# A two-layer hybrid encoder trunk on one core: four plain tiles in the channel mixers, with low parts of weights made by accumulating transfers

## The chip, the core and the metric

The kernel runs on one core of a Trainium2 chip. The core has a matrix engine (TensorE, "PE" in the profile, with its weight loads as "PEld"), a vector engine (VectorE, DVE), a scalar engine (ScalarE, ACT), a general engine (GpSimd, POOL) and a queue engine (SyncE, SP). Each runs its instructions in the order in which they stand, and they wait for each other on semaphores. Transfers are issued by SP, ACT or POOL and carried out by 16 DMA engines. The metric is device time in microseconds (us) of one execution; lower is better.

## What is computed

Batch 1, 512 tokens, width 1024, two layers, everything in float32. A layer is a token mixer and a channel mixer, each added to x. The part that matters here is the channel mixer, once per layer, and the final norm:

```python
def conv_ffn(h, w_up, conv_w, conv_b, w_down):        # h = rmsnorm(x, norm_ffn_g[l]), 512 x 1024
    u, g = jnp.split(h @ w_up, 2, axis=-1)            # w_up 1024 x 5632: u and g are 512 x 2816
    g = causal_dwconv(g, conv_w, conv_b)              # three taps along the tokens
    return (jax.nn.silu(g) * u) @ w_down              # w_down 2816 x 1024

x = x + conv_ffn(rmsnorm(x, norm_ffn_g[l]), ffn_w_up[l], ...)
...
return rmsnorm(x, final_g)                            # after the last layer
```

The first layer's token mixer is an mLSTM with memory attention, the second's a band attention with memory attention; neither is touched.

## The kernel before

Matrices are kept transposed: 128 features on the partitions, 512 tokens along the free axis. To reach float32 accuracy with a single-pass matmul type, each operand is split into a high part and a low part (`split`: ACT copies the high part, DVE subtracts it from the source), and each product is three matmuls (`mm3`, L194 to L196): high weights with high data, high weights with low data, low weights with high data. The low part of the weights is thus first needed by the third matmul.

The up projection's 2816 channels are 22 tiles of 128. Each has a "gate" and an "up" half, each with weights of 1024 x 128, loaded by SP into one of three raw buffers (`wr`), split into one of three pairs of buffers (`wh0`/`wl0` to `wh2`/`wl2`, here buffers 0, 1, 2; `weight_tiles` hands them out in turn, and `turn` may be moved on to skip some). There are two ways to do a tile:

- A *plain* tile (`plain`) multiplies all 8 feature blocks over all 512 tokens: 2 x 8 x 3 matmuls of 512 columns. The first three plain tiles use data that isn't yet scaled by the norm, and DVE scales the result by a row (L718); later ones use scaled data. Then come the three taps (ACT L692, DVE L685 twice), a Silu (L722), the product with the up half (L727) and the split of the result, which is kept in `hid`.
- A *block* tile (`step`) treats gate and up, and two halves of features and tokens, as a 2 x 2 block product in seven products of 256 columns instead of eight: 7 x 4 x 3 matmuls of 256 columns. It needs sums and differences of the data (`forms`, made once per mixer in four steps, one for each pair of feature blocks) and of the weights (`Forms`, made for each tile: `sums`, `split_second`, `sum_third` and so on).

The down projection is accumulated in DRAM in groups of four tiles of `hid` (`GROUP`): a *down unit* is 4 x 3 matmuls of 512 columns for one block of output features. Its sum is copied out of PSUM by ACT and added into `xspill` in DRAM by a transfer that accumulates (L778, issued by POOL). `UNITS` says which units are done beside which tile.

Before, tiles 0 to 4 are plain, and units 0 to 3 follow the fifth plain tile. The steps of `forms` (scaling of x, its splits, then the four sums) are woven into the plain tiles by `weave`, which calls the next step each time so many matmul triples have been written. All this is written in program order and then ordered by a scheduler; the block tiles after it stand under a manual schedule for PE, ACT and DVE, in the order written in `step`.

At the end of the program the second mixer's last six tiles are multiplied with the tokens on the partitions, and for each group T of 128 tokens `final_norm` scales the rows by the inverse root of their mean square (one Newton step after a square root) and issues two output transfers, one from ACT's queue and one from SP's.

Of the kernel before, what the change touches and what calls it, by code (L numbers as in the profile page):

```python
# [13 lines left out]
ALU = mybir.AluOpType  # L14
# [25 lines left out]

PLAIN, UNSCALED, GROUP, LAST = 5, 3, 4, 6
UNITS = {PLAIN - 1: (0, 1, 2, 3), 5: (None, 4), 6: (None, 5), 7: (None, 6), 8: (None, 7)}
UNITS.update((j, (2 * j - 10, 2 * j - 9)) for j in range(9, 21))

# [8 lines left out]
def trunk(  # L55
# [139 lines left out]
        nc.tensor.matmul(o, lh, rl, start=False, stop=False, skip_group_check=more)  # L195
        nc.tensor.matmul(o, ll, rh, start=False, stop=last, skip_group_check=more)  # L196

    def project(w, c0, act, tag="mm"):


        n = len(act)
        wh, wl = weights(rows(w, c0, P), n, P)
        o = ps(tag)
        for k in range(n):
            mm3(o, wh[:, k, :], wl[:, k, :], act[k][0], act[k][1], k == 0, k == n - 1)
            yield
        return o
# [457 lines left out]
    class ChannelMixer:  # L665
# [35 lines left out]
        def plain(self, j):  # L701
            scale = self.norm.row if j < UNSCALED else None
            act = self.act if j < UNSCALED else self.ready
            gate = project(self.w, DFF + j * P, act)
            up = project(self.w, j * P, act, "sc")
            if self.norm.row is None:
                both = pair_of(gate, up)
                weave(self.norm.finish(), both, 1)
                og, ou = yield from both
                scale = self.norm.row  # L710
            else:
                og = yield from gate
# [12 lines left out]
            if ou is None:  # L725
                ou = yield from up
            V.tensor_tensor(out=acc, in0=ou, in1=acc, op=ALU.mult)  # L727
            self.keep(acc)

        def forms(self):  # L730

            for j in range(KT):
                V.scalar_tensor_tensor(
                    xT[j], xT[j], self.gain[:, j : j + 1], self.norm.row, op0=ALU.mult, op1=ALU.mult
                )
                hi, lo = sb("u", [P, S], F32R), sb("u", [P, S], F32R)
                split(hi, lo, xT[j])
                self.ready.append((hi, lo))
                yield
            self.sums = []  # L740
            for k in range(KT // 2):
                b1, b2 = xT[k], xT[k + KT // 2]
                forms = []
                ta, tb = sb("t", [P, S]), sb("t", [P, S])
                for o, x, y in (
                    (ta[:, :H], b1[:, H:], b1[:, :H]),
                    (ta[:, H:], b2[:, H:], ta[:, :H]),
                    (tb[:, :H], b2[:, H:], b1[:, H:]),
                    (tb[:, H:], b2[:, :H], ta[:, H:]),
                ):  # L750
                    V.tensor_tensor(out=o, in0=x, in1=y, op=ALU.subtract)
                for t in (ta, tb):
                    for h in (t[:, :H], t[:, H:]):
                        both = sb("u", [P, S], F32R)
                        split(both[:, :H], both[:, H:], h)
                        forms.append(both)
                self.sums.append(forms)
                yield

# [6 lines left out]
        def down_products(self, u):  # L766
            g, j = divmod(u, KT)
            w = self.down[u // 2]
            o = ps("tr")
            c = slice(u % 2 * P, (u % 2 + 1) * P)  # L770
            for k in range(GROUP):
# [28 lines left out]

        def t(self, i):

            return [(p[i - 1][:, :H], p[i - 1][:, H:]) for p in self.sums]

        def later(self):


            prep, tail = Forms(self, PLAIN), None
            prep.split_up()
            prep.sums()  # L810
            prep.split_second()
            prep.sum_third()
            prep.split_sums()
            prep.sum_fourth()
# [619 lines left out]
    def add_squares(T, t):  # L1434

        if len(sums[T]) == 1:
            V.tensor_scalar(sums[T][0], sums[T][0], 1.0 / D, EPS, op0=ALU.mult, op1=ALU.add)
        elif sums[T]:
            last = sums[T].pop()
            V.scalar_tensor_tensor(sums[T][0], last, 1.0 / D, sums[T][0], op0=ALU.mult, op1=ALU.add)  # L1440
        sums[T].append(small(1))
        sq = sb("t", [P, S])
        A.activation(sq[:, : t.shape[-1]], t, AF.Square, accum_out=sums[T][-1])

    def final_norm(T):
        v, r, t = small(1), small(1), small(1)
        first, second = sums[T]
        A.activation(r, second, AF.Sqrt, scale=1.0 / D, bias=first)
        V.scalar_tensor_tensor(v, second, 1.0 / D, first, op0=ALU.mult, op1=ALU.add)
        V.reciprocal(r, r)  # L1450
        V.tensor_mul(t, r, r)
        V.scalar_tensor_tensor(t, t, -0.5, v, op0=ALU.mult, op1=ALU.mult)
        V.scalar_tensor_tensor(r, t, 1.5, r, op0=ALU.add, op1=ALU.mult)
        A.activation(xt[T][0], xt[T][0], AF.Copy, scale=r)
        nc.scalar.dma_start(out[T * P : (T + 1) * P, :S], xt[T][0])
        V.scalar_tensor_tensor(xt[T][1], xt[T][1], r, fgb[1], op0=ALU.mult, op1=ALU.mult)
        nc.sync.dma_start(out[T * P : (T + 1) * P, S:], xt[T][1])

    hid = channel_mixer(1, act, norm, col["gffn"][:, 8:16], lambda: None)
    n = LAST // 2  # L1460
# [77 lines left out]
```

## Time and profile before

| | us |
|---|---|
| median of 3 timed runs | 1179.51 (1179.32 to 1180.14) |
| profiled execution: its own time | 1181.13 |
| profiled execution: span from first to last instruction | 1179.4 |
| PE busy in that span | 1167.9 |
| DVE busy | 941.3 |
| ACT busy | 730.0 |
| POOL busy | 129.7 |

Rows of the timeline read: start, busy time, engine, line, operation, tiles written and read, shapes; in brackets the idle time before and what ended it. Matmuls are pipelined, so their starts tell the pace and not their lengths. Where a source line is a helper's (L140 and L141 are the two steps of `split`), the tiles and the place in time tell which use it is. `pmm`, `psc`, `ptr` are PSUM buffers; plain gates write `pmm`, plain ups `psc`, down units `ptr`.

### The profile page before, as it was taken

What the parts mean: (1) busy time and instruction counts of PE and PEld (TensorE: products, weight loads), DVE (VectorE), ACT (ScalarE), POOL (GpSimd) and SP (SyncE); (2) the same over time, 40 slices, a digit from 0 to 9 for tenths busy, and PEclk for the clock granted to TensorE, in tenths of its full rate; (3) what the DMA queues carried; (4) which work ended last, traced back from release to release, by engine and by line L of the source; (5) the groups of instructions that cost most, each with busy time, mean ns of one, the idle gap of its engine ahead of it and who ended that gap; (6) DMA issues with size and microseconds to landing.
All of it is one profiled execution on the core that took longest, in us unless ns stands there. A gap on an engine that the chain in (4) does not pass through costs nothing.

```text
span 1179.4 us, 18657 instructions
## 1 busy us (share of the span) xinstructions
PE 1167.9 (99%) x7007; PEld 1033.9 (88%) x7007; DVE 941.3 (80%) x1688; ACT 730.0 (62%) x1294; POOL 129.7 (11%) x222
## 2 busy tenths in 40 slices
PE   8999999999999999999999999999999999999997
PEld 8988888888889999999888888888889999999986
DVE  5877778787979877777697888897897887777755
ACT  5638578654656665556576667776565665666545
POOL 0211101000011111111021000101001011110100
PEclk9999999999999999999999999999999999999999
DMA  8645425244366866666564312335426466566551
GB/s 283 206 116 132 105 54 152 66 136 134 90 155 146 189 157 171 151 154 136 146 196 134 90 54 80 105 104 179 143 90 152 109 137 143 142 143 143 126 161 72
DMA packets 200156, 158.64 MB, mean 135 GB/s; under 512 B 8344, under 2 KB 179838, under 8 KB 200066
## 3 DMA queue, kind: packets, MB, share of 16 engines
q1 hardware_dynamic: 183906, 119.74, 34.7%
q0 software_dynamic: 15584, 36.67, 15.7%
q8 instruction: 55, 0.90, 0.3%
q10 hardware_dynamic: 576, 1.05, 0.2%
q14 instruction: 35, 0.29, 0.1%
HBM read 128.89 MB, written 32.46 MB: 137 GB/s over the span
## 4 chain that ended last, share of the span: by engine, by line
PE 93%; DVE 3%; DMA 2%; ACT 1%; SPq 1%; issue 0%; POOL 0%; POOLq 0%; ACTq 0%; DVEq 0%
PE pmm L194 18%; PE pmm L195 18%; PE pmm L196 18%; PE ptr L195 6%; PE ptr L194 6%; PE ptr L196 6%; PE psc L196 5%; PE psc L195 5%; PE psc L194 5%; PE psc L544 2%; PE ptr L1365 1%; DMA wr<-in_mem_w_kv_dram 1%; PE ptr L1386 1%; PE ptr L1387 1%; DMA u<-in_mem_dram 1%; PE ptr L627 1%
## 5 line engine op out<-in xcount | busy, mean ns | idle before, releaser
L194 PE MATMUL pmm<-u,wh 128*128 128x512 f32 (+1 forms) x968 | 333.0, 344 | 0.2 <-ACT u L140 0.2
L196 PE MATMUL pmm<-u,wl 128*128 128x512 f32 (+1 forms) x968 | 330.7, 342 | 0.0
L195 PE MATMUL pmm<-u,wh 128*128 128x512 f32 (+1 forms) x968 | 330.4, 342 | 0.0
L141 DVE TENSOR_TENSOR wl<-wr,wh 128x1024 fp32r<-128x1024 f32 (+3 forms) x172 | 199.9, 1163 | 81.6 <-ACT wh L140 81.2
L140 ACT CAST wh<-wr 128x1024 fp32r<-128x1024 f32 (+3 forms) x172 | 171.9, 1001 | 93.3 <-PE pmm L195 40.3
L196 PEld LDWEIGHTS pmm<-u,wl 128*128 128x128 f32 x968 | 181.9, 188 | 20.7
L194 PEld LDWEIGHTS pmm<-u,wh 128*128 128x128 f32 x968 | 181.8, 188 | 18.8 <-ACT u L140 1.1
L195 PEld LDWEIGHTS pmm<-u,wh 128*128 128x128 f32 x968 | 182.0, 188 | 18.4 <-DVE u L141 0.5
L194 PE MATMUL ptr<-u,wh 128*128 128x512 f32 x272 | 106.4, 391 | 0.0
L195 PE MATMUL ptr<-u,wh 128*128 128x512 f32 x272 | 106.2, 390 | 0.0
L196 PE MATMUL ptr<-u,wl 128*128 128x512 f32 x272 | 105.8, 389 | 0.0
L778 POOL DMA_DIRECT2D xspill<-t x64 | 55.5, 867 | 432.6 <-ACT t L777 420.1
L834 ACT COPY t<-pmm 128x256 f32<-128x256 f32 x102 | 38.2, 374 | 76.6 <-PE pmm L196 76.5
L141 DVE TENSOR_TENSOR u<-t,u 128x512 fp32r<-128x512 f32 (+1 forms) x94 | 54.3, 604 | 35.4 <-ACT u L140 35.4
L194 PE MATMUL pmm<-u,fh 128*128 128x256 f32 x272 | 75.4, 277 | 0.0
L195 PE MATMUL pmm<-u,fh 128*128 128x256 f32 x272 | 75.2, 277 | 0.0
L196 PE MATMUL psc<-u,wl 128*128 128x256 f32 (+1 forms) x232 | 75.1, 324 | 0.0
L196 PE MATMUL pmm<-u,fl 128*128 128x256 f32 x272 | 75.1, 276 | 0.0
L195 PE MATMUL psc<-u,wh 128*128 128x256 f32 (+1 forms) x232 | 75.1, 324 | 0.0
L194 PE MATMUL psc<-u,wh 128*128 128x256 f32 (+1 forms) x232 | 74.9, 324 | 0.0
L141 DVE TENSOR_TENSOR fl<-pt,fh 128x512 fp32r<-128x512 f32 x102 | 70.3, 689 | 5.1 <-ACT fh L140 1.4
L140 ACT CAST fh<-pt 128x512 fp32r<-128x512 f32 x102 | 62.9, 616 | 8.8 <-DVE pt L888 5.6
(335 smaller groups left out, 2510.4 us busy)
## 6 DMA issues: line engine op xcount, KB each, us to landing
wr<-in_ffn_w_up_dram SPq DMA_DIRECT2D x54, 512.0 KB, 6.5
wr<-in_ffn_w_down_dram SPq DMA_DIRECT2D x38, 512.0 KB, 5.3
pt<-in_ffn_w_up_dram SPq DMA_DIRECT2D x34, 512.0 KB, 8.0
xspill<-t POOLq DMA_DIRECT2D x64, 256.0 KB, 4.5
wr<-in_a_w_in_dram SPq DMA_DIRECT2D x20, 512.0 KB, 3.9
wr<-in_w_kv_dram SPq DMA_DIRECT2D x12, 512.0 KB, 4.1
xspill<-fh POOLq DMA_DIRECT2D x16, 256.0 KB, 2.6
xspill<-fl POOLq DMA_DIRECT2D x16, 256.0 KB, 2.8
```

The costliest lines, as they stand in the source:

```text
L140: high = A.copy(hi, src) if on_act else V.tensor_copy(hi, src)
L141: low = V.tensor_tensor(out=lo, in0=src, in1=f(hi), op=ALU.subtract)
L194: nc.tensor.matmul(o, lh, rh, start=first, stop=False, skip_group_check=more)
L195: nc.tensor.matmul(o, lh, rl, start=False, stop=False, skip_group_check=more)
L196: nc.tensor.matmul(o, ll, rh, start=False, stop=last, skip_group_check=more)
L544: nc.tensor.matmul(o, a, b, start=first and i == 0, stop=i == 1)
L627: nc.tensor.matmul(o2, vs[a][:, 2 * hp + h, :], p[h][:, a, :], start=i == 0, stop=i == 3)
L778: G.dma_start(xspill[j], t, accum_op=ALU.add)
L834: A.copy(o, r[:, :H])
L1365: nc.tensor.transpose(tp[:, b * P : (b + 1) * P], es[T, h][:, b * P : (b + 1) * P], ident)
L1386: nc.tensor.matmul(o2[:, s * P :], w, hi_at(pts[h], s, s, TT - s), start=s == 0, stop=False)
L1387: nc.tensor.matmul(o2[:, s * P :], w, lo_at(pts[h], s, s, TT - s), start=False, stop=s == TT - 1)
```

## The change

Five things change in the channel mixers and at the end:

1. `PLAIN` goes from 5 to 4: tile 4 becomes a block tile. Units 0 to 3 now follow tile 3, and tile 4 has no unit beside it.
2. For plain tiles 2 and 3 (gate and up, so four weight tiles a mixer), the low part is made by `added`: ACT copies the high part, then writes its negative into the low buffer, and POOL issues a transfer that reads the weights from DRAM a second time and adds them there. The raw buffer is free once the high part is copied.
3. Units 0 and 1 do their first three parts at once and their fourth, which needs tile 3's own result, later.
4. The last of the four sums of x is made after the first parts of tile 4's weights (`run(forms)` moves into `later`), and the results of the sums are split in 512 columns at a time instead of 256.
5. `final_norm` uses one small DVE step fewer, and the last group's rows are scaled and sent in two halves, three of the four transfers by SP.

The turn of the buffers changes too: `turn` is moved on once, ahead of tile 2.

```diff
-PLAIN, UNSCALED, GROUP, LAST = 5, 3, 4, 6
+PLAIN, UNSCALED, GROUP, LAST = 4, 3, 4, 6
...
+    def added(src, a, b):
+
+        hi, lo = weight_tiles(a, b)
+        A.copy(hi, load(src, a, b))
+        A.activation(lo, f(hi), AF.Copy, scale=-1.0)
+        G.dma_start(lo, src.bitcast(F32R), accum_op=ALU.add)
+        return hi, lo
+
-    def project(w, c0, act, tag="mm"):
+    def project(w, c0, act, tag="mm", split_by=weights):
...
-        wh, wl = weights(rows(w, c0, P), n, P)
+        wh, wl = split_by(rows(w, c0, P), n, P)
...
-            gate = project(self.w, DFF + j * P, act)
-            up = project(self.w, j * P, act, "sc")
+            gate, up = (
+                project(self.w, c0 + j * P, act, tag, added if j >= 2 else weights) for c0, tag in ((DFF, "mm"), (0, "sc"))
+            )
...
-                    for h in (t[:, :H], t[:, H:]):
-                        both = sb("u", [P, S], F32R)
-                        split(both[:, :H], both[:, H:], h)
-                        forms.append(both)
+                    hi, lo = sb("u", [P, S], F32R), sb("u", [P, S], F32R)
+                    split(hi, lo, t)
+                    forms += [(hi[:, c], lo[:, c]) for c in (slice(0, H), slice(H, S))]
...
-        def later(self):
+        def later(self, forms):
...
             prep.split_second()
+            run(forms)
             prep.sum_third()
...
-        skips = -(turn[0] + 1) % 3
+        skips = -(turn[0] + 2) % 3
         for j in range(1, UNSCALED):
-            turn[0] += j <= skips
+            turn[0] += skips * (j == UNSCALED - 1)
...
-            weave(mixer.plain(j), forms, 4 / (16.0 * (PLAIN - UNSCALED)))
+            weave(mixer.plain(j), forms, 3 / (16.0 * (PLAIN - UNSCALED)))
+            started = {}
             for u in units:
...
-                mixer.add(*mixer.down_products(u))
-        run(forms)
-        mixer.later()
+                if u < 2:
+                    started[u] = mixer.down_products(u, 0, GROUP - 1)[1]
+                if u == 1:
+                    for v, o in started.items():
+                        mixer.add(*mixer.down_products(v, GROUP - 1, GROUP, o))
+                if u >= 2:
+                    mixer.add(*mixer.down_products(u))
+        mixer.later(forms)
...
-        V.tensor_mul(t, r, r)
-        V.scalar_tensor_tensor(t, t, -0.5, v, op0=ALU.mult, op1=ALU.mult)
-        V.scalar_tensor_tensor(r, t, 1.5, r, op0=ALU.add, op1=ALU.mult)
...
+        V.scalar_tensor_tensor(t, r, v, r, op0=ALU.mult, op1=ALU.mult)
+        V.scalar_tensor_tensor(r, t, 3.0, r, op0=ALU.add, op1=ALU.mult)
+        step = S if T < TT - 1 else MEM
+        for c in range(0, S, step):
+            a, b = (t[:, c : c + step] for t in xt[T])
+            last = c + step == S
+            A.activation(a, a, AF.Copy, scale=r)
+            V.scalar_tensor_tensor(b, b, r, fgb[1][:, c : c + step], op0=ALU.mult, op1=ALU.mult)
+            nc.sync.dma_start(out[T * P : (T + 1) * P, S + c : S + c + step], b)
+            (nc.scalar if last else nc.sync).dma_start(out[T * P : (T + 1) * P, c : c + step], a)
```

How the instructions move is seen at two places of the first mixer. The digit after `wh` or `wl` is the buffer. On ACT, from the Silu of tile 0 on, before (`wh1613` is tile 2's gate, `wh0635` tile 3's gate, `wh2623` tile 2's up):

```order
L722 ACTIVATE t588_3033<-t588_3033 128x512
L140 CAST wh1613_3143<-wr612_3141 128x1024
L140 CAST u590_3042<-t588_3033 128x512
L140 CAST wh0635_3240<-wr634_3238 128x1024
L692 ACTIVATE t600_3087<-t601_3088,cols1_799 128x512
L140 CAST u596_3066<-fh448_2360 128x512
L140 CAST u598_3083<-fh449_2362 128x512
L140 CAST wh2623_3192<-wr622_3190 128x1024
L722 ACTIVATE t600_3087<-t600_3087 128x512
```

and now, the same stretch (`wh0612` is tile 2's gate, `wh1622` its up):

```order
L731 ACTIVATE t588_3033<-t588_3033 128x512
L201 CAST wh0612_3141<-wr614_3143 128x1024
L202 ACTIVATE wl0613_3142<-wh0612_3141 128x1024
L140 CAST u590_3042<-t588_3033 128x512
L700 ACTIVATE t600_3087<-t601_3088,cols1_799 128x512
L140 CAST u596_3066<-fh448_2360 128x512
L140 CAST u598_3083<-fh449_2362 128x512
L140 CAST u606_3115<-fh450_2364 128x512
L731 ACTIVATE t600_3087<-t600_3087 128x512
L140 CAST u608_3132<-fh451_2366 128x512
L201 CAST wh1622_3191<-wr624_3193 128x1024
L202 ACTIVATE wl1623_3192<-wh1622_3191 128x1024
```

Tile 3's gate no longer has its copy here. It stands further down, and its negative copy (`wl2637`) behind tile 2's tap (L700 on `t620`):

```order
L140 CAST u626_3212<-fl454_2372 128x512
L201 CAST wh2636_3244<-wr638_3246 128x1024
L700 ACTIVATE t620_3183<-t621_3184,cols1_799 128x512
L140 CAST u628_3229<-fl455_2374 128x512
L202 ACTIVATE wl2637_3245<-wh2636_3244 128x1024
L731 ACTIVATE t620_3183<-t620_3183 128x512
L201 CAST wh0647_3295<-wr649_3297 128x1024
L202 ACTIVATE wl0648_3296<-wh0647_3295 128x1024
```

The accumulating transfers follow each negative copy on POOL's queue, with nothing else between them; behind them come the down units' own. On PE, at the end of tile 1's up (`psc605`) and the start of tile 2's gate (`pmm615`), before:

```order
L194 MATMUL psc605_3101<-u571_2950,wh2603_3097 128x512
L195 MATMUL psc605_3101<-u572_2951,wh2603_3097 128x512
L196 MATMUL psc605_3101<-u571_2950,wl2604_3098 128x512
L194 MATMUL pmm615_3147<-u538_2794,wh1613_3143 128x512
L195 MATMUL pmm615_3147<-u539_2795,wh1613_3143 128x512
L196 MATMUL pmm615_3147<-u538_2794,wl1614_3144 128x512
```

and now:

```order
L194 MATMUL psc605_3101<-u571_2950,wh1603_3097 128x512
L195 MATMUL psc605_3101<-u572_2951,wh1603_3097 128x512
L196 MATMUL psc605_3101<-u571_2950,wl1604_3098 128x512
L194 MATMUL pmm615_3148<-u538_2794,wh0612_3141 128x512
L195 MATMUL pmm615_3148<-u539_2795,wh0612_3141 128x512
L196 MATMUL pmm615_3148<-u538_2794,wl0613_3142 128x512
```

The order of the matmuls is the same there; the buffers and what fills them are not. Tile 1's gate is in buffer 1 before and in buffer 0 now, so in both programs tile 2's gate takes the buffer that tile 1's gate has just left.

More of the change, by code (lines that the diff above doesn't have):

```diff
@@ L764, in load_down, with down_products @@
             return load(rows(ffn_w_down[self.l], 2 * jj * P, 2 * P, GROUP * g, GROUP * (g + 1)), GROUP, 2 * P)
-        def down_products(self, u):
+        def down_products(self, u, k0=0, k1=GROUP, o=None):
             g, j = divmod(u, KT)
             w = self.down[u // 2]
-            o = ps("tr")
+            o = o or ps("tr")
             c = slice(u % 2 * P, (u % 2 + 1) * P)
-            for k in range(GROUP):
+            for k in range(k0, k1):
                 mm3(o, w[0][:, k, c], w[1][:, k, c], *self.hid[GROUP * g + k], k == 0, k == GROUP - 1)
@@ L801, in t @@
         def t(self, i):
-            return [(p[i - 1][:, :H], p[i - 1][:, H:]) for p in self.sums]
-        def later(self):
+            return [p[i - 1] for p in self.sums]
+        def later(self, forms):
             prep, tail = Forms(self, PLAIN), None
@@ L1436, in add_squares @@
         if len(sums[T]) == 1:
-            V.tensor_scalar(sums[T][0], sums[T][0], 1.0 / D, EPS, op0=ALU.mult, op1=ALU.add)
+            V.tensor_scalar(sums[T][0], sums[T][0], 4.0 / D, 4 * EPS, op0=ALU.mult, op1=ALU.add)
         elif sums[T]:
             last = sums[T].pop()
-            V.scalar_tensor_tensor(sums[T][0], last, 1.0 / D, sums[T][0], op0=ALU.mult, op1=ALU.add)
+            V.scalar_tensor_tensor(sums[T][0], last, 4.0 / D, sums[T][0], op0=ALU.mult, op1=ALU.add)
         sums[T].append(small(1))
@@ L1447, in final_norm @@
         first, second = sums[T]
-        A.activation(r, second, AF.Sqrt, scale=1.0 / D, bias=first)
-        V.scalar_tensor_tensor(v, second, 1.0 / D, first, op0=ALU.mult, op1=ALU.add)
+        A.activation(r, second, AF.Sqrt, scale=4.0 / D, bias=first)
+        V.scalar_tensor_tensor(v, second, -4.0 / D, first, op0=ALU.mult, op1=ALU.subtract)
         V.reciprocal(r, r)
-        V.tensor_mul(t, r, r)
-        V.scalar_tensor_tensor(t, t, -0.5, v, op0=ALU.mult, op1=ALU.mult)
-        V.scalar_tensor_tensor(r, t, 1.5, r, op0=ALU.add, op1=ALU.mult)
[L1454 to L1457, printed above, removed]
+        V.scalar_tensor_tensor(t, r, v, r, op0=ALU.mult, op1=ALU.mult)
[8 more added lines that the diff above has]
+            (nc.scalar if last else nc.sync).dma_start(out[T * P : (T + 1) * P, c : c + step], a)
     hid = channel_mixer(1, act, norm, col["gffn"][:, 8:16], lambda: None)
```

## The prediction

> **What bounds the kernel now.** I read the page first, then the busy time by stages, then the timelines at the places where the change works. The page's first part and its chain of waits:
>
> ```profile
> span 1179.4 us, 18657 instructions
> PE 1167.9 (99%) x7007; PEld 1033.9 (88%) x7007; DVE 941.3 (80%) x1688; ACT 730.0 (62%) x1294; POOL 129.7 (11%) x222
> PE 93%; DVE 3%; DMA 2%; ACT 1%; SPq 1%; issue 0%; POOL 0%; POOLq 0%; ACTq 0%; DVEq 0%
> ```
>
> TensorE (PE) carries the span. A busy PE need not run at its peak, so here are stages of the first channel mixer (its tiles 0 to 2; tiles 3 and 4 with the four early down units; the blocks) and the end of the program. The columns are length, then busy time of PE, its weight loads, DVE, ACT and POOL, the granted clock, the DMA share and GB/s.
>
> ```profile
> 282.60:309.80 27.20, 27.20 (x122) 22.51 (x121) 26.54 (x38) 17.88 (x26) 0.00 (x0) 1.00 0.32 96
> 309.80:342.60 32.80, 32.80 (x145) 26.93 (x144) 30.18 (x58) 19.78 (x37) 2.59 (x3) 1.00 0.42 110
> 342.60:582.00 239.40, 239.40 (x1764) 225.39 (x1763) 190.76 (x275) 143.86 (x243) 39.42 (x53) 1.00 0.65 154
> 1172.20:1179.40 7.20, 0.19 (x2) 0.00 (x0) 2.05 (x9) 1.52 (x4) 0.00 (x0) 0.82 0.38 146
> ```
>
> The mixers leave PE no idle time. The matmuls also start at an even pace, which the timeline of PE shows: first a stretch of 512-column matmuls (24 for each weight tile, two weight tiles a plain tile), then of 256-column ones (84 a block).
>
> ```profile
> 298.90 0.39 PE L194 MATMUL pmm<-u,wh 128*128 128x512 f32 x1
> 299.13 0.39 PE L195 MATMUL pmm<-u,wh 128*128 128x512 f32 x1
> 299.35 0.39 PE L196 MATMUL pmm<-u,wl 128*128 128x512 f32 x1
> ...
> 304.34 0.39 PE L194 MATMUL psc<-u,wh 128*128 128x512 f32 x1
> ...
> 309.78 0.39 PE L194 MATMUL pmm<-u,wh 128*128 128x512 f32 x1
> ...
> 320.66 0.39 PE L194 MATMUL pmm<-u,wh 128*128 128x512 f32 x1
> ...
> 342.61 0.28 PE L194 MATMUL pmm<-u,wh 128*128 128x256 f32 x1
> ...
> 345.33 0.28 PE L194 MATMUL pmm<-u,fh 128*128 128x256 f32 x1
> ```
>
> From 298.90 to 304.34 lie 24 matmuls: 0.2267 us each. From 342.61 to 345.33 lie 24 of the narrow kind: 0.1133 each. So only two things move the time inside the mixers: the number of columns that PE streams, and any wait that the change brings in. There is no wait to take out.
>
> **Columns.** A plain tile is 48 x 0.2267 = 10.88 us, a block 84 x 0.1133 = 9.52. One tile of each of the two mixers changes from the one to the other: 2 x 1.36 = **2.72 us less**. The four early down units keep their 48 matmuls and only move one tile earlier.
>
> **The accumulating transfers.** For tiles 2 and 3 the low part no longer comes from DVE in one step. ACT writes the high part, then its negative, and POOL's queue adds the raw weights from DRAM. DVE loses four 1024-column steps a mixer, ACT gains four; neither is on PE's path, since PE ran without a gap beside them. What counts is when the low part is there: the third matmul of a weight tile needs it (L196). So the latency of the transfer, from issue to landing, stands on PE's path wherever the buffer comes free late. In the new order tile 2's gate of the first mixer takes buffer 0, last read by tile 1's gate, with one weight tile (5.44 us) between them. Before, it took buffer 1, last read by the same distance, but its chain was short. That wait for the buffer is in the trace of before, on ACT:
>
> ```profile
> 293.43 1.05 ACT L140 CAST wh<-wr 128x1024 fp32r<-128x1024 f32 x1 [1.05 <-PE pmm L195]
> ...
> 295.38 1.05 ACT L140 CAST wh<-wr 128x1024 fp32r<-128x1024 f32 x1
> 296.34 0.81 ACT L692 ACTIVATE t<-t,cols 128x512 f32<-128x512 f32 x1
> 297.05 1.12 ACT L140 CAST u<-fh 128x512 fp32r<-128x512 f32 x2
> ```
>
> A copy of 1024 columns holds ACT 0.96 us (295.38 to 296.34), the tap 0.71, a copy of 512 some 0.56. Let L be the latency of one transfer. High copy from 293.43, negative copy behind it, 0.1 to issue: 295.45. The low part lands at 295.45 + L, the matmul starts 0.1 later; today it starts at 299.35. The first wait is therefore L - 3.8. The remaining 22 matmuls take 4.99, so the gate ends at 300.5 + L. Now the second place: on ACT the negative copy for tile 3's gate stands behind tile 2's tap, which needs that gate's sum scaled by DVE. DVE's steps of 512 columns follow each other every 0.60 us, and its low part of 1024 takes 1.14:
>
> ```profile
> 336.86 0.68 DVE L888 TENSOR_TENSOR pt<-wr,pt 128x512 f32<-128x512 f32 x1
> 337.46 0.69 DVE L141 TENSOR_TENSOR fl<-pt,fh 128x512 fp32r<-128x512 f32 x1
> 338.22 1.23 DVE L141 TENSOR_TENSOR wl<-pt,wh 128x1024 fp32r<-128x1024 f32 x1
> 339.36 0.69 DVE L141 TENSOR_TENSOR fl<-pt,fh 128x512 fp32r<-128x512 f32 x1
> ```
>
> From the gate's end: 0.25 to DVE, 0.60, 0.1, tap 0.71, one copy 0.56, negative copy 0.96, 0.1 to issue, together 3.3; then L again. Tile 3's gate gets its third matmul at 303.9 + 2L. The rest of tile 3 is 44 matmuls, 9.97 us, so the tile ends at 313.9 + 2L instead of 320.66. **The first mixer loses 2L - 6.8 us** (tile 2's up part becomes late by under 1 us, inside that second wait). Queued behind it are the early down units and the whole block stage, which PE runs in order. POOL has nothing else in that stretch (0.00 above), so its queue adds no wait.
>
> The second mixer has a kinder rotation: there tile 2's gate takes the buffer of tile 0's up, and tile 2's up that of tile 1's gate. Its places on the timelines:
>
> ```profile
> 847.18 1.06 ACT L140 CAST wh<-wr 128x1024 fp32r<-128x1024 f32 x1 [1.05 <-PE pmm L195]
> ...
> 852.65 0.39 PE L194 MATMUL pmm<-u,wh 128*128 128x512 f32 x1
> ...
> 869.42 0.39 PE L196 MATMUL psc<-u,wl 128*128 128x512 f32 x1
> ```
>
> Tile 2's up: free at 847.18, issued two ACT steps later at 849.2, needed at 852.65 + 5.44 + 0.45 = 858.5: room for L up to 9.3, and the gate's the same. Tile 3's gate waits for the buffer until 852.65, then for a Silu and its copies: issued near 856.8, needed at 864.0, room 7.1. Tile 3's up is the tightest: its raw weights load into the buffer that the copy before has freed (855.7, and 3.8 for a load, below), then copy, tap, copy, negative copy: issued near 862.9, needed at 869.42, room 6.5.
>
> L itself has no row, since before nothing accumulates into SBUF. The nearest rows are a lone accumulating transfer of 256 KB to DRAM in 2 KB rows (window 906 to 911) and a lone plain load of 512 KB in 512-byte rows, the very shape wanted (296 to 301). In each the queue's line gives packets, MB and the share of 16 engines over 5 us, and the issue's line the time to landing.
>
> ```profile
> q0 software_dynamic: 144, 0.26, 41.8%
> ...
> xspill<-t POOLq DMA_DIRECT2D x1, 256.0 KB, 4.0
> ```
>
> ```profile
> q1 hardware_dynamic: 1040, 0.52, 35.9%
> ...
> wr<-in_ffn_w_up_dram SPq DMA_DIRECT2D x1, 512.0 KB, 3.8
> ```
>
> The lower end is 3.8, adding for free. The accumulating one held the engines 0.418 x 80 = 33.4 us, 2.1 on each, so 1.9 of its 4.0 is fixed. Twice the bytes at that rate: 4.2 + 1.9 = 6.1. If instead each packet cost what those did (33.4 / 144 = 0.232), 1040 of them would be 15.1 + 1.9 = 17.0, the upper end. I go by bytes, since the plain load's small packets were cheap (0.359 x 80 / 1040 = 0.028 each), and add 0.3 because the next raw load (1.8 us on each engine) starts about when the transfer does: **L = 6.4**. So the first mixer loses 2 x 6.4 - 6.8 = **6.0 us**, the second nothing.
>
> The Trainium skill, "DMA: Bandwidth & Descriptors", section on the anatomy of one DMA on the SWDGE path, fits such a transfer as 2.0 us plus bytes over 436 GB/s. For 512 KB an estimate from it is 3.2 us, at which the first wait vanishes and the sum is near rival A below. The row of 256 KB disagrees: 4.0 measured, 2.6 by the page, which does not speak of accumulation there; the row decides.
>
> **The seam to the blocks.** In the plain stage DVE has 26.5 of 27.2 and 30.2 of 32.8 us to do. It loses four low parts (4.6) and one tile's work (two low parts, two taps, three steps: some 5.4), and the stage 10.9, so its share stays near 95%: it keeps pace, without slack. After tile 3's last matmul PE now has only the first three parts of units 0 and 1, 18 x 0.2267 = 4.1 us, then two matmuls of the block, 0.2, ahead of the first that needs the block's low part (in the first mixer two more unit matmuls, 0.45). On ACT and DVE stand until then: copy 0.96, copy 0.56, DVE 0.60, the down unit's low part 1.14, 0.60, the block's low part 1.14, together 5.0. Waits of 0.3 and 0.7, **+1.0 us**; bounds 0, if the order gives, and 2.5, if DVE comes late by one tap chain. Units 2 and 3 (5.4 us of PE) cover x's last sum behind them, so its new place costs nothing; without that cover it would be 2.5 us of DVE. The sums' splits in 512 columns instead of 256 save DVE some 0.6 us a mixer, off PE's path. The first block without a down unit (9.5 us) asks some 8 us of DVE: no wait. The block tile's other DMAs only start one tile sooner.
>
> **The end.** DVE's last steps after the last matmul:
>
> ```profile
> 1173.75 0.16 DVE L1450 RECIPROCAL s<-s 128x1 f32<-128x1 f32 x1 [0.17 <-ACT s L1448]
> 1173.95 0.16 DVE L1451 TENSOR_TENSOR s<-s 128x1 f32<-128x1 f32 x1
> ...
> 1174.53 0.75 DVE L1456 SCALAR_TENSOR_TENSOR u<-u,s,bias 128x512 f32<-128x512 f32 x1
> 1175.28 0.37 ACTq L1455 DMA_DIRECT2D out_dram<-u  x1
> ```
>
> One small step less saves 0.20. The last rows are scaled and written in halves: the first half leaves 0.4 us earlier, but SP's queue now holds three issues of about 0.35 instead of one, so its last one goes out some 0.2 later, with half the bytes. I take **-0.1**, bounds -0.5 and +0.3.
>
> **Sum.** -2.7 + 6.0 + 1.0 - 0.1 = +4.2 us on the span. The profiled execution's span is 1179.4 us and its own time 1181.13; the median of the three timed runs is 1179.51. The difference carries over: **1183.7 us**.
>
> **Rivals.** A, *the transfers land almost as fast as plain loads*. For it speaks that the source rows are cheap when plain; against it, that the 256 KB row is already slower than 512 KB plain. At L = 3.8 to 4.3 the first mixer loses 0.8 to 1.8, and with the seam at 0 to 1.0 the time is 1177.5 to 1179.5: not slower. L = 4.3 is where it decides. B, *the packets are the cost*: at L = 8 the first mixer loses 9.2 and the second 1.5 (8 less its room of 6.5), +9 us or 1188.5; at 10 it is 1194, at 17 some 1215. For it speaks 0.232 us a packet; against it that those are four times as long. C, *PE slows after the waits*: the two waits are 2.6 and 2.8 us. The only idle stretch in the trace is the end, where the clock's mean of 0.82 over 7.2 us puts half speed in the last 2.6 us, so 4.6 us of idling passed first. If each wait of mine brought half speed for as long as it lasted (no row tells how long), that would add 2.7: 1186.4. The Trainium skill, "TensorE: Matmul & The Clock Gate", part 1, has the clock fall after an idle window of about 3.4 us and return after as long; an estimate from that is 1.7 a fall, 1187.1, and the end row, with its 4.6, does not contradict it. D, *no wait at all*, the copies find their buffers free earlier than I read: 1179.5 - 2.8 = 1176.7.
>
> **How the numbers follow.** Timings of this kernel tell apart about 0.2%, 2.4 us. My case, L from 4.9 to 7.6 (1181 to 1187), has 0.6; A 0.15, B 0.1, C 0.08, D 0.07. Faster by over 0.2% (under 1177.1) is D: 0.07. Within 0.2% are A and the part of my case with L under 5.5: 0.23. Slower: 0.7. The range reaches from A's lower end, 1177.5, to B at a little over 8, 1189.5.
>
> **What would show it.** In the new trace, PE must idle ahead of an L196 in tile 2's gate and tile 3's gate of the first mixer, each 2 to 4 us, released by a DMA; the second mixer must be clean or nearly so there. The transfers on POOL's queue must land near 6.4 us. PE's 256-column matmuls grow by 168. I am wrong if these transfers land near 4 us, if the second mixer waits as long as the first, or if the blocks, not the plain tiles, hold the waits.

## The result, and the profile after

The changed kernel takes 1196.6 us (median of 4 runs, 1196.23 to 1196.92) against 1179.72 for the kernel before (4 runs, 1179.32 to 1180.14): a ratio of 1.0143, interval 1.0131 to 1.0156. It is slower by 16.9 us, where 4.2 were forecast, and lies 7 us above the range's upper end. The page of the profile, its first part:

```profile
span 1195.1 us, 18833 instructions
PE 1174.2 (98%) x7079; PEld 1039.5 (87%) x7079; DVE 942.9 (79%) x1681; ACT 740.7 (62%) x1301; POOL 141.3 (12%) x230
```

Where does the loss lie? A landmark in each mixer is the pair of matmuls that sums the squares for the norm, just before tile 0's up part. Timeline of PE, before (first two rows) and after (last two):

```profile
281.41 0.63 PE L299 MATMUL psc<-t,onesr 128*128 128x512 f32 x2
...
835.15 0.63 PE L299 MATMUL psc<-t,onesr 128*128 128x512 f32 x2
```

```profile
279.48 0.63 PE L307 MATMUL psc<-t,onesr 128*128 128x512 f32 x2
...
847.37 0.63 PE L307 MATMUL psc<-t,onesr 128*128 128x512 f32 x2
```

From one landmark to the other it was 553.74 and is 567.89: **14.15 us more in the first mixer's part**. From the second landmark to the end of the span it was 344.25 and is 347.73: **3.5 more in the second's**. (Up to the first landmark the profiled execution of before was 1.9 longer, which is why the spans differ by less than these two together.)

In the first mixer the waits of PE, grouped by what ended them, are these; each line gives the sum, the count and the longest. First 296 to 372 us, then the same place in the second mixer, 860 to 915:

```profile
PE pmm L196 <- DMA wl<-in_ffn_w_up_dram: 6.9, 2, 3.8
PE psc L194 <- DVE t L863: 0.9, 1, 0.9
PE pmm L196 <- DVE wl L141: 0.6, 1, 0.6
PE pmm L194 <- ACT t L843: 0.5, 1, 0.5
```

```profile
PE psc L194 <- DVE t L863: 0.9, 1, 0.9
PE pmm L195 <- DVE u L141: 0.6, 1, 0.6
PE psc L196 <- DMA wl<-in_ffn_w_up_dram: 0.6, 1, 0.6
PE pmm L194 <- ACT t L843: 0.5, 1, 0.5
```

The two large waits stand where the prediction put them: at the third matmul of tile 2's gate and of tile 3's gate in the first mixer, ended by the accumulating transfer. The timeline of PE there:

```profile
297.20 0.39 PE L195 MATMUL pmm<-u,wh 128*128 128x512 f32 x1
300.69 0.80 PE L196 MATMUL pmm<-u,wl 128*128 128x512 f32 x1 [3.11 <-DMA wl<-in_ffn_w_up_dram]
301.29 0.63 PE L194 MATMUL pmm<-u,wh 128*128 128x512 f32 x1
301.71 0.63 PE L195 MATMUL pmm<-u,wh 128*128 128x512 f32 x1
...
306.73 0.39 PE L195 MATMUL pmm<-u,wh 128*128 128x512 f32 x1
306.95 0.40 PE L196 MATMUL pmm<-u,wl 128*128 128x512 f32 x1
...
314.72 0.40 PE L195 MATMUL psc<-u,wh 128*128 128x512 f32 x1
318.90 0.50 PE L196 MATMUL pmm<-u,wl 128*128 128x512 f32 x1 [3.79 <-DMA wl<-in_ffn_w_up_dram]
```

From start to start, less one matmul of 0.227, the waits are 3.26 and 3.95 us. But behind the first the matmuls follow every 0.42 us (301.29 to 301.71) instead of every 0.22 (306.73 to 306.95). The stages' table shows the granted clock, the third number from the end: half, in two stretches of 6.8 and 3.5 us. Whether the clock is the cause is tested below.

```profile
299.70:306.50 6.80, 5.81 (x14) 4.55 (x15) 2.13 (x4) 3.61 (x6) 1.55 (x1) 0.50 0.98 178
...
320.00:323.50 3.50, 3.50 (x10) 2.69 (x9) 2.51 (x5) 0.62 (x1) 0.00 (x0) 0.53 1.30 208
```

The other waits stand in the first block tile (tile 4). At about 350 us PE waits for ACT's copy (L843) and then for DVE's addition (L863); both return in the second mixer. Ahead of them PE waits, in the first mixer, for the block's first low part (`wl`, at 336 us), and in the second for the low part of x's last sum (`u`, at 904 us). In the later blocks PE has no wait, neither before nor now.

### The profile page after: what moved, and what is told of

The parts are those of the page before. It is cut to its first block, busy times and chain, and to the rows that moved or that the text cites. A ratio compares the mean times of both kernels' runs of the same rounds, so it can differ in the third digit from the quotient of the medians.

```text
span 1195.1 us, 18833 instructions
## 1 busy us (share of the span) xinstructions
PE 1174.2 (98%) x7079; PEld 1039.5 (87%) x7079; DVE 942.9 (79%) x1681; ACT 740.7 (62%) x1301; POOL 141.3 (12%) x230
## 4 chain that ended last, share of the span: by engine, by line
PE 87%; DVE 5%; issue 4%; ACT 3%; DMA 1%; POOL 0%; DVEq 0%; POOLq 0%; ACTq 0%
PE pmm L194 17%; PE pmm L196 17%; PE pmm L195 17%; PE ptr L195 6%; PE ptr L194 6%; PE ptr L196 6%; PE psc L194 4%; PE psc L195 4%; PE psc L196 4%; PE psc L552 2%; PE ptr L1380 1%; DVE u L141 1%; PE ptr L1401 1%; ACT wh L140 1%; PE ptr L1402 1%
## 5 line engine op out<-in xcount | busy, mean ns | idle before, releaser
L141 DVE TENSOR_TENSOR wl<-wr,wh 128x1024 fp32r<-128x1024 f32 (+4 forms) x162 | 187.7, 1159 | 76.6 <-ACT wh L140 76.2
L140 ACT CAST wh<-wr 128x1024 fp32r<-128x1024 f32 (+4 forms) x162 | 161.3, 997 | 86.6 <-PE pmm L195 41.1
L194 PEld LDWEIGHTS pmm<-u,wh 128*128 128x128 f32 x976 | 184.5, 189 | 18.5 <-ACT u L140 1.1
L195 PEld LDWEIGHTS pmm<-u,wh 128*128 128x128 f32 x976 | 184.5, 189 | 18.4 <-DVE u L141 0.5
L141 DVE TENSOR_TENSOR u<-t,u 128x512 fp32r<-128x512 f32 x78 | 53.9, 691 | 41.5 <-ACT u L140 41.5
L843 ACT COPY t<-pmm 128x256 f32<-128x256 f32 x108 | 40.3, 374 | 73.9 <-PE pmm L196 73.8
L194 PE MATMUL pmm<-u,fh 128*128 128x256 f32 x288 | 80.2, 278 | 1.1 <-ACT t L843 1.0
L195 PE MATMUL pmm<-u,fh 128*128 128x256 f32 x288 | 79.8, 277 | 0.6 <-DVE u L141 0.6
L196 PE MATMUL pmm<-u,fl 128*128 128x256 f32 x288 | 79.6, 276 | 0.0
L141 DVE TENSOR_TENSOR fl<-pt,fh 128x512 fp32r<-128x512 f32 x108 | 74.4, 690 | 4.8 <-ACT fh L140 1.0
L196 PE MATMUL psc<-u,wl 128*128 128x256 f32 (+1 forms) x224 | 71.1, 318 | 0.6 <-DMA wl<-in_ffn_w_up_dram 0.6
L195 PE MATMUL psc<-u,wh 128*128 128x256 f32 (+1 forms) x224 | 71.1, 317 | 0.0
L194 PE MATMUL psc<-u,wh 128*128 128x256 f32 (+1 forms) x224 | 71.0, 317 | 0.0
```

Of the source, the lines that this page charges most:

```text
L140: high = A.copy(hi, src) if on_act else V.tensor_copy(hi, src)
L141: low = V.tensor_tensor(out=lo, in0=src, in1=f(hi), op=ALU.subtract)
L194: nc.tensor.matmul(o, lh, rh, start=first, stop=False, skip_group_check=more)
L843: A.copy(o, r[:, :H])
```

## The experiments

The first four take the changed kernel and alter one thing each. They ran on one chip, where the kernel before took 1179.47 (7 runs). On every chip used here it took 1179.3 to 1179.7, so times are compared across them.

**The rotation of the weight buffers.**

```diff
-            turn[0] += skips * (j == UNSCALED - 1)
+            turn[0] += skips * (j == 1)
```

> The changed kernel with one edit: the turn of the weight buffers is moved on ahead of tile 1 instead of tile 2, which gives the first mixer the second mixer's rotation (tile 2's gate takes the buffer of tile 0's up). Theory 'late buffers': PE's two waits in the first mixer (3.3 and 4.0 us at tile 2's and tile 3's gate, with some 4.4 us of matmuls at half pace behind them) come from buffers that are free too late for a latency of 6.7 us; with the other rotation the first mixer loses what the second loses there, 0.7 us. So 11.7 - 0.7 = 11 us less: 1185.6. Rival 'the transfers cost wherever they stand' (in the first mixer something else is late, say the data or the norm): little changes, 1194 to 1197. Between, 1190, if only one of the two waits goes.

Measured: 1188.24 (1188.04 to 1188.48), ratio 1.0073 [1.0056, 1.0090], so 8.4 less than the changed kernel. The three longest waits of PE in the first mixer:

```profile
PE pmm L196 <- DVE wl L141: 1.1, 1, 1.1
PE psc L307 <- ACT t L140: 0.8, 1, 0.8
PE psc L194 <- DVE t L863: 0.8, 1, 0.8
```

No wait for a transfer is left, and no stretch at half clock. So the transfers' waits came from buffers that were free too late. In the first mixer the edit does more than I had expected: tile 2's gate gets a buffer that is free even before tile 0's up, not the one that tile 0's up leaves. Its transfer is issued at 280.2 us, where the changed kernel has 294.0. The missing 2.6 us have their place too. The norm's matmuls now wait for ACT (with what follows, 1.6 us), since tile 2's two copies (L201 at 276.75, L202 at 278.85) stand ahead of the norm's (279.80). The first block's low part comes later, and in the first mixer PE now waits 0.6 for x's last sum.

**The transfers taken out.**

```diff
-                project(self.w, c0 + j * P, act, tag, added if j >= 2 else weights) for c0, tag in ((DFF, "mm"), (0, "sc"))
+                project(self.w, c0 + j * P, act, tag, weights) for c0, tag in ((DFF, "mm"), (0, "sc"))
```

> The changed kernel without the accumulating transfers: tiles 2 and 3 get their low parts from DVE again, all else as changed, the rotation too. Theory 'late buffers': the first mixer's waits and the half pace go (11.7 us), and the second's 0.7; DVE, which had 94% of its time filled in this stage, pays some of the 4.6 us a mixer back at the seam, 0 to 2 us each: 1184 to 1188. Rival 'DVE bound': the four low parts are what DVE can no longer carry beside four plain tiles, and it is 4 us late at the first block in each mixer: 1192 or more.

Measured: 1184.65 (1184.12 to 1184.81), ratio 1.0042 [1.0027, 1.0057]; 12 less than with them. DVE carries the four low parts again and PE waits no longer for it than before: the plain tiles run without a gap. What the transfers relieved was not what PE waited for. Yet the kernel is still 5.2 us slower than before, although it streams 2.7 us less of columns. Some 8 us must lie at the seam; from start to start its trace shows 4.3 there in the first mixer and 3.0 in the second.

**x's last sum back in the plain tile.**

```diff
-            weave(mixer.plain(j), forms, 3 / (16.0 * (PLAIN - UNSCALED)))
+            weave(mixer.plain(j), forms, 4 / (16.0 * (PLAIN - UNSCALED)))
...
+        run(forms)
         mixer.later(forms)
...
-            run(forms)
             prep.sum_third()
```

> The changed kernel with x's last sum back inside the last plain tile (four sums woven into it, none left for later). Theory 'the last sum's place': in the first block of each mixer PE waits 0.7 and 1.0 us because ACT makes that sum's high parts only after it has copied out the down units, and DVE idles 3.2 us for them; with the sum back these waits go, and the 2.5 us of DVE time that return ahead of the first block's parts are covered by the plain tile: about 2 x 1.7 less, 1193. Rival 'DVE without slack': the sum ahead of the block's weights makes these later by up to 2.5 us in each mixer, and the waits in the block stay or shrink: 1196 to 1200.

Measured: 1198.47 (1197.75 to 1199.38), ratio 1.0160 [1.0145, 1.0176]; 1.9 more than the changed kernel. My theory fell; the time lies in the rival's range. The two waits in the first block are as they were, and the block's low part is later (PE waits 1.8 for it here and 2.1 in the second mixer, where the changed kernel has 0.6 and some 0.3). Waits of PE in the first mixer:

```profile
PE pmm L196 <- DMA wl<-in_ffn_w_up_dram: 6.3, 2, 3.5
PE pmm L196 <- DVE wl L141: 1.8, 1, 1.8
PE psc L196 <- DMA wl<-in_ffn_w_up_dram: 1.1, 1, 1.1
PE psc L194 <- DVE t L862: 0.9, 1, 0.9
PE pmm L194 <- ACT t L842: 0.5, 1, 0.5
```

The wait for x's last sum is gone, but the later low part costs more, and behind it the clock falls once more (last section). So the sum's later place helps on balance, and something else makes PE wait in the first block.

**PE kept busy in the two waits.**

```diff
+        for _ in range(extra):
+            nc.tensor.matmul(o, wh[:, 0, :], act[0][0], start=True, stop=False, skip_group_check=True)
         for k in range(n):
             mm3(o, wh[:, k, :], wl[:, k, :], act[k][0], act[k][1], k == 0, k == n - 1)
...
+                    {2: 13, 3: 16}.get(j, 0) if self.l == 0 and c0 else 0,
```

> The changed kernel with idle work for PE in the first mixer's two waits: 13 and 16 more matmuls of 512 columns ahead of tile 2's and tile 3's gate (their result is overwritten), 2.9 and 3.6 us, a little less than the waits. The waits themselves stay. Theory 'the clock': the matmuls at 0.427 us pitch behind each wait (some 2.7 and 1.7 us lost) come from PE's idling; kept busy, it goes on at 0.227 and the time falls by 4.4: 1192.2. Rival 'contention' (the slow pace comes from the transfers or the weight loads in that stretch): the pace stays slow, 1196 to 1198.

Measured: 1192.92 (1192.63 to 1193.29), ratio 1.0113 [1.0098, 1.0128]; 3.7 less, with 29 matmuls more. The clock stays up through the whole stretch:

```profile
296.90:326.00 29.10, 28.14 (x124) 22.74 (x123) 20.36 (x36) 18.43 (x26) 4.61 (x3) 1.00 0.82 143
```

So the slow pace was the clock, lowered by PE's own idling, and not contention: the transfers are the same (DMA share 0.82, and 0.83 over the same stretch of the changed kernel, where the mean clock is 0.82). Part of the gain was given back, since tile 2's up now waits 1.0 us for its own transfer.

The next four ran on another chip (kernel before: 1179.54, 21 runs). The question was the seam.

**The kernel before, its first block without a down unit.**

```diff
-UNITS = {PLAIN - 1: (0, 1, 2, 3), 5: (None, 4), 6: (None, 5), 7: (None, 6), 8: (None, 7)}
+UNITS = {PLAIN - 1: (0, 1, 2, 3), 6: (None, 4), 7: (None, 5), 8: (6, 7)}
```

> The kernel before with one edit: its first block tile (tile 5) has no down unit beside it; units 4 to 7 stand beside tiles 6, 7 and, both, 8. The work is the same. Theory 'the first block needs a unit': without one, PE runs from the third sum product straight into the fourth, which writes the same PSUM buffer, and waits for ACT to copy the third out (0.7 us) and then for DVE to read the other buffer behind a low part of 1024 columns (1.0); with the pauses of 0.1 behind each, 1.9 in each mixer: 1179.5 + 3.8 = 1183.3. Rival 'throughput' (the prediction's reading: 9.5 us of PE ask 8 of DVE, no wait): 1179.5.

Measured: 1183.73 (1183.04 to 1183.90), ratio 1.0034 [1.0022, 1.0046]: 4.2 slower with the same work. In each mixer the two waits appear that the changed kernel has, and no others at the seam. The first mixer's:

```profile
PE psc L194 <- DVE t L854: 0.9, 1, 0.9
PE pmm L194 <- ACT t L834: 0.5, 1, 0.5
```

In `step`, the third sum product writes a PSUM buffer that ACT must copy out before the fourth product may write it (L834), and the last product needs the other buffer, which DVE reads (L854) only behind a low part of 1024 columns. A unit's 12 matmuls stand between and hide both. Without one they are bare: 1.9 us a mixer from start to start, some 4 in the kernel.

**Each transfer in two halves** (changed kernel).

```diff
-        G.dma_start(lo, src.bitcast(F32R), accum_op=ALU.add)
+        for c in (slice(0, a // 2), slice(a // 2, a)):
+            G.dma_start(lo[:, c], src[:, c].bitcast(F32R), accum_op=ALU.add)
```

> The changed kernel with each accumulating transfer sent as two, one for each half of the feature blocks (256 KB, 512 packets each). The third matmul needs the first half alone, the second half is needed 2.7 us later. Theory 'latency in a late rotation': the loss follows the latency of the first piece, twice, and the clock stays up once the waits are short. With some 4.6 us from issue to landing for the first half, 2.1 less than 6.7, the waits of 3.3 and 4.0 become 1.2 and 1.9 and the 4.4 us at half pace go: 8.6 less, 1188.0. Rival 'fixed cost': a half lands hardly sooner, or the second is late by as much: 1195 to 1198.

Measured: 1192.03 (1190.97 to 1194.32), ratio 1.0101 [1.0084, 1.0118]; 4.6 less instead of 8.6. The first halves for the gates did land after 4.6 to 4.8 us in the first mixer. But the halves queue behind each other:

```profile
L204 POOL DMA_DIRECT2D wl<-in_ffn_w_up_dram x16: 1263/1570/1862, 294.4 to 872.6; - x16
...
DMA to landing us min/median/max: 4.6/5.8/7.4
```

Columns of the first line are least, median and greatest ns on POOL: two halves hold POOL longer (1.3 and 1.8 us) than one whole (1.5). The gates wait for 1.9 us in all, the ups, whose transfers come behind, for 3.4:

```profile
PE psc L196 <- DMA wl<-in_ffn_w_up_dram: 3.4, 2, 2.5
PE pmm L196 <- DMA wl<-in_ffn_w_up_dram: 1.9, 2, 1.2
```

The gates' part of the loss follows the latency: 1.9 us, where 3.1 were expected. What I had left out was the queue. The theory also had the clock stay up. In the profiled execution (1194.32) it did not: behind the wait of 2.5 at tile 3's up the granted clock is 0.52 from 321.0 to 324.4. And in the second mixer PE waits 1.6 for the first block's low part; why it came so late was not followed up.

**A unit beside tile 4** (without the accumulating transfers: the edit on `project` above is made too).

```diff
-UNITS = {PLAIN - 1: (0, 1, 2, 3), 5: (None, 4), 6: (None, 5), 7: (None, 6), 8: (None, 7)}
-UNITS.update((j, (2 * j - 10, 2 * j - 9)) for j in range(9, 21))
+UNITS = {PLAIN - 1: (0, 1, 2, 3), **{j: (None, j) for j in range(4, 10)}}
+UNITS.update((j, (2 * j - 10, 2 * j - 9)) for j in range(10, 21))
```

> The changed kernel without accumulating transfers (low parts of tiles 2 and 3 by DVE) and with a down unit beside tile 4: units 4 to 9 stand singly beside tiles 4 to 9, all else as changed. Theory 'the first block needs a unit': of the version without transfers (1184.65) the waits of 0.7 and 1.0 in block 4 go in both mixers, 3.8: 1180.9. Rival 'it only moves': the unit needs its weights split one tile sooner, one more copy of ACT and 1.1 us of DVE at the seam, and block 9, whose two units become one, has waits instead: 1183 to 1186.

Measured: 1180.73 (10 runs, 1180.41 to 1183.51), ratio 1.0011 [1.0001, 1.0020]; 3.9 less than without the unit, as expected. The two waits are gone in both mixers. What is left at the seam is the wait for the first low part (0.6 and 0.5) and, in the first mixer, one of 0.7 for ACT's copy of the block's first product (L851).

**A third unit started early** (on top of the last).

```diff
-                if u < 2:
-                    started[u] = mixer.down_products(u, 0, GROUP - 1)[1]
-                if u == 1:
+                if u < 3:
+                    started[u] = mixer.down_products(u, 0, GROUP - 1, ps("mm") if u == 2 else None)[1]
+                if u == 2:
...
-                if u >= 2:
+                if u >= 3:
```

> The kernel with low parts by DVE and a unit beside tile 4, and one step more: three units instead of two do their first three parts ahead of tile 3's own result, the third in a free buffer of pmm; so 2 us of PE's work more stand ahead of the first block. Theory 'the seam is a chain, not a lack of DVE time': the block's low part is then there in time, and the 0.7 us that PE waited for it in each mixer go (with the pauses behind, 1.8): 1179.1. Rival 'DVE without slack': the waits move behind the units, to x's last sum, and the time stays at 1181.

Measured: 1177.06 (10 runs, 1176.53 to 1178.19), ratio 0.9977 [0.9968, 0.9987]: **faster than the kernel before by 2.5 us**, and 2.0 below the expectation, because the other waits and pauses went as well: from start to start PE lost 2.4 and 1.6 us at the seam in the version before this one, and now 0.4 and 0.1. In its stages (plain tiles, then units and first blocks of the first mixer; all of that in the second) PE is busy throughout, at full clock:

```profile
279.60:321.40 41.80, 41.80 (x186) 34.60 (x185) 39.55 (x63) 25.44 (x37) 0.00 (x0) 1.00 0.31 93
321.40:360.00 38.60, 38.60 (x277) 35.59 (x276) 34.33 (x54) 23.68 (x41) 8.27 (x11) 1.00 0.59 140
836.00:900.00 64.00, 64.00 (x347) 55.38 (x346) 60.70 (x97) 38.43 (x60) 4.32 (x5) 1.00 0.46 120
```

DVE is busy for 39.55 of 41.80 us in the first row, with the four low parts back on it, and PE loses nothing beside it. So a lack of DVE time did not make PE wait; the seam's waits were single chains without cover. What remains of the change on PE's path is the block in a plain tile's place (2.7 us less, by the forecast) and the shorter end.

The last two ran on that chip as well (kernel before: 1179.33, 21 runs).

**The transfers put back into the mended version** (the two edits above on `project` and `turn`, the first undone, the second made).

> The fastest version so far (1177.1: low parts by DVE, a unit beside tile 4, three units started early) with the accumulating transfers put back for tiles 2 and 3, in the second mixer's rotation, so that each has room for 6.7 us. Theory 'transfers with room are free': no wait in the plain tiles; they bring nothing either, since PE has no wait left that DVE's time could shorten: 1177, up to 1178.7 if the rotation again puts ACT's copy for tile 1 ahead of the norm's parts (1.6 us in the version with the rotation alone). Rival 'they disturb': ACT's two copies for each weight tile and POOL's queue make other steps late, 1181 or more.

Measured: 1180.24 (10 runs, 1179.16 to 1181.10), ratio 1.0004 [0.9995, 1.0013]; 3.2 more than without them. No wait for a transfer worth counting, as the first theory had it, but more than it allowed. Waits of PE in the first mixer:

```profile
PE ptr L195 <- DVE u L141: 1.2, 1, 1.2
PE psc L307 <- ACT t L140: 0.6, 1, 0.6
PE psc L307 <- DVE t L141: 0.2, 1, 0.2
```

The norm's wait is the one seen with the rotation alone, again behind tile 2's copies. The other is new: two low parts of 1024 columns (from 324.03 and 325.76) now stand ahead of tile 3's own low part on DVE, and the units wait for it. From start to start the two cost 2.9 us. Whether another order would make the transfers free was not tried.

**The end alone** (kernel before with the new `add_squares` and `final_norm`, as in the change's diff).

> The kernel before with the changed end alone (one small DVE step less, the last rows scaled and sent in halves, three of four transfers by SP). The profiles put the span's end 7.29 us after the start of the last matmul before and 6.95 after; so 0.3 us less, 1179.2, which the timing alone cannot tell from nothing. Rival: with four issues in a row instead of two the last transfer goes out later and the end is 0.3 longer, 1179.8.

Measured: 1179.13 (11 runs, 1178.65 to 1180.31), ratio 0.9997 [0.9988, 1.0006]: no difference that the timing can tell. In its profile the span ends 6.96 us after the start of the last matmul, 7.29 before.

## Why the prediction was wrong, point by point

- **Columns, -2.7.** Right as far as it can be seen: the version without waits is 2.5 faster, the end included. PE's matmuls grew by 72, which is 168 narrow ones more and 96 wide ones less.
- **L = 6.4.** Right, in its parts too: the eight transfers took 6.3 to 9.3 us, median 6.7. From 290 to 330 us four of them filled POOL's queue for 42.2% of the engines' time, 4.2 us each, as I had it by bytes; what is left is 2.5 where I had 1.9 and 0.3. (My row of 256 KB was not quite alone: a raw load was issued 1.1 us behind it.)

```profile
L203 POOL DMA_DIRECT2D wl<-in_ffn_w_up_dram x8: 1530/1544/1612, 294.0 to 875.7; - x8
...
DMA to landing us min/median/max: 6.3/6.7/9.3
```

  Rival A, and the estimate of 3.2 from the Trainium skill's "DMA: Bandwidth & Descriptors" (anatomy of one DMA on the SWDGE path), are refuted by this row; so is rival B, with 4160 packets at 0.065 us each in that stretch against its 0.232.
- **The first mixer loses 2L - 6.8.** The mechanism was right. With L = 6.7 it gives 6.6; the waits were 3.26 + 3.95 = 7.2. The other 0.6 lie ahead of the two issues: 2.4 us from the free buffer to the first (forecast 2.0), and 3.5 from the gate's end to the second (3.3). The lateness of tile 2's up did not show, since the slow clock held its gate back; with PE kept busy it waited its 1.0 us.
- **Rival C, given 0.08, came on top of it.** This is the first step that failed. I left it out of the sum because I set the waits (2.6 and 2.8) beside the end's 4.6 us of idling, as if that were a threshold. It is none: the clock halved after 3.3 and 4.0 us here, and after 2.0 in the version with the last sum back. By the pitch of the matmuls this cost 4.4 us, by the run with PE kept busy 3.7, the wait of tile 2's up already paid; I had priced it at 2.7. The Trainium skill, "TensorE: Matmul & The Clock Gate", part 1, says that the clock follows windows of about 3.4 us that run freely. The trace agrees: the half-clock stretches of 6.8 and 3.5 us are two windows and one, and their ends (the matmuls' pitch returns at 306.4 and 323.5) lie 17.1 apart, five windows. So the 1.7 a fall that I worked out from it is the price of one window only, and the first fall lasted two.
- **The second mixer loses nothing.** Nearly: 0.6 us at tile 3's up (with the pause behind it 0.8), the place that I had called the tightest. Its transfer was issued at 875.7, 0.6 later than I had it: its raw weights landed 0.4 later, and POOL issued 0.3 instead of 0.1 after the copy.
- **The seam, +1.0.** This is the second step that failed, by most. From start to start PE lost 3.1 us there in the first mixer and 3.8 in the second. The sentence "The first block without a down unit (9.5 us) asks some 8 us of DVE: no wait" compared sums of busy time, where chains decide: product, copy by ACT, product in the same buffer, and the like for the other buffer, which DVE reads behind a low part. They cost 1.9 in each mixer, and taking the unit from the first block of the kernel before shows the same 4 us with the same work. The rest is 1.2 and 1.9. The block's first low part costs 0.8 and 0.3 of it (forecast 0.3 and 0.7: that these add up alike is luck). x's last sum, for which I had nothing, costs 0.8 in the second mixer, though in its old place the kernel was 1.9 slower. What is left are pauses of 0.1 to 0.2.
- **The end, -0.1.** It was -0.3 in the profiles, within its bounds.
- **Sum.** -2.7 + 7.2 + 0.8 + 4.4 + 6.9 - 0.3 = 16.3 of the 16.9 us. The remaining 0.6 was not traced; it may be pauses under 0.1 that I did not add up, and the spread of single executions.

"Wrong if the blocks, not the plain tiles, hold the waits" has come half true: the plain tiles hold 12.4 us of the loss and the seam 6.9.

## What to carry to other kernels

A throughput balance ("8 us of work in 9.5") says nothing about a stage whose steps write the same buffer one after another: follow one buffer from its last reader to its next writer, and ask what stands between them on the waiting engine. When work is moved out of a stage, ask first what it was hiding there. And a wait of 2 to 4 us on TensorE can cost more than itself: these runs show seven such waits in the channel mixers (3.3 and 4.0; 3.0, 3.6, 2.0 and 2.3; 2.7 from start to start), and behind all but those of 3.6 and 2.3 the clock fell. A forecast of one needs the clock's fall in its sum, not only among the rivals.

## What the runs showed of the hardware that I had not expected

The clock's fall goes by where the idle time lies, not by its length alone. In the version with the last sum back, a wait of 3.6 us (from 314.8) left the clock up, as the first row below shows for the 14.6 us behind it, and one of 2.0 (334.7 to 336.7) was followed within 0.3 us by half clock:

```profile
318.40:333.00 14.60, 13.49 (x58) 10.85 (x59) 10.84 (x21) 8.21 (x13) 0.00 (x0) 1.00 0.49 89
334.70:336.70 2.00, 0.22 (x2) 0.04 (x1) 2.00 (x4) 0.00 (x0) 0.00 (x0) 1.00 0.28 68
337.00:340.40 3.40, 3.40 (x13) 2.83 (x12) 1.41 (x3) 1.62 (x3) 1.00 (x2) 0.54 0.82 245
```

If the windows are those of 3.4 us, one need not be wholly idle, which differs from the "idle window" of the Trainium skill ("TensorE: Matmul & The Clock Gate", part 1) as I read it. An explanation would be that the long wait was split by a window's border into two parts too short, and the short one lay within a single window. The times allow it: in this trace the clock returns near 306.5 and 340.7, ten windows apart. Counted from there a border falls near 316.8, inside the long wait (parts of some 1.9 and 1.7), and none inside the short one. But 1.9 and 2.0 lie close together, this is argued from the times, and no run was made for it. In the second mixer of the same run a wait of 2.3 us (from 893.1) left the clock up too.

An accumulating transfer of 512 KB in 512-byte pieces held POOL for 1.5 us and landed after 6.7, where a plain load of the same shape on SP's queue landed after 3.8 before the change.
